# Changed order of preference in the crossing and in attention, and conditioning strips summed through DRAM, in a two-layer hybrid backbone step

## Chip, cores and metric

One core of one Trainium2 chip runs the whole program. The metric is device time in microseconds, from launch to end on that core; a value for a kernel is the median of its runs.

## The reference, cut to what matters

A step of a diffusion backbone over 256 context tokens and 1024 latent tokens of width 1024, two layers: gated linear attention in both directions (GLA), then softmax attention with eight query heads and two key heads. Both layers are modulated by a conditioning vector (`c` for the latent tokens, `c_ctx` for the context):

```python
for l in range(DEPTH):
    mod_p = (jax.nn.silu(c_ctx) @ w_ada[l] + b_ada[l])[None, None, :]
    mod_s = (jax.nn.silu(c) @ w_ada[l] + b_ada[l])[:, None, :]
    sh_p, sc_p, gt_p = split_mod(mod_p)
    sh_s, sc_s, gt_s = split_mod(mod_s)
    hp = rms_norm(xp, norm_g[l]) * (1.0 + sc_p) + sh_p
    hs = rms_norm(xs, norm_g[l]) * (1.0 + sc_s) + sh_s
    ...                      # l = 0: gla_mixer; l = 1: softmax attention, latent keys + cached keys
    xp = xp + gt_p * out_p
    xs = xs + gt_s * out_s
```

So each layer needs 3 x 1024 conditioning values for two vectors: shift, scale and gate.

## The kernel before

All large products are made in three passes of half-precision matmuls (high x high, high x low, low x high; `mm3`, L155), over tiles of 128 tokens. The stages, by the time in the profile:

- **Front** (0 to about 50 us): `x` and 8 MB of `w_ada` come in, the first layer's shift and scale are made (`cond_vectors`, `mod_rows`, `affine(0)`), the first tokens normalised, transposed and modulated into `hT_hi` and `hT_lo`.
- **GLA** (to about 582 us): `gla` runs 50 slots, five rounds (`h` 0 to 4) of ten token tiles. A slot makes a head's decay, states and local products for one tile, the projections ahead (`value_gate`, `qk_piece`), finishes the head before (`combine`, `gated`), and calls `filler(slot)`, which hangs on the rest: the stages of later weights, the conditioning blocks, from slot 30 the output weights, and from slot 42 the first four output tiles. Start and final states and, before, the gate strips share the one tile `s0`.
- **Crossing** (to about 723 us, `gla_out`): output projection and `residual` of the other tiles, the second layer's modulation (`mod_tile`, with rows `gb` from DRAM), keys and values (`key_tile`), first query tiles (`query`, `query_rest`). Each projected tile first needs its row prepared: `out_prep` scales it, splits it and transposes it by DMA into `hT_hi` and `hT_lo`.
- **Attention** (to about 1171 us): ten steps (`n`), each four heads of 256 tokens; the scores of a head come in two halves (`scores` j = 0, 1) over PSUM tile `S`; ScalarE's exponential `p` (L1189), high and low parts `phl`, a DMA transpose into `PT`, and two heads later `values`. Query tiles, their finishing, key tiles and gates lie between.
- **Output** (to the end): `att_out`, the second output projection and its residuals.

**The conditioning blocks.** The 16 blocks of 256 columns that the front leaves over (the first layer's gate, all of the second layer) are loaded at odd slots; the slot after, `gemv` makes eight products in four 32-row strips of the PE array, so the result `m` (128 x 256) holds four partial sums, two rows of each strip being used. The slot after that, `mod_sum` adds the strips on PE against the 0/1 matrix `sel` (L335 for shift and scale, L345 for gates), and VectorE adds the bias (L337, L346); gates go to DRAM (`gt_d`, L347). `affine(1)` at slot 34 scales the second layer's shift and scale, and `affine_rows` transposes them (L372) and stores them (`gb_d`). They are read at slot 40, as rows broadcast to all partitions.

**What sets the order.** The program is written by one thread; a planner then orders each engine's instructions with a timeline of its own. Each instruction has a place in the order of writing, and of the instructions that are ready in that timeline the one with the lowest place goes first. `with k.later("name")` adds `LATER["name"]` to the places of what is written in it: a positive number puts it behind, a negative one ahead. `tc.issue_after(x)` puts instructions behind `x` on its engine. The order planned is fixed in the program; the engines run it in that order and wait where something is late.

Of the kernel before, what the change touches and what calls it, by code (L numbers as in the profile page):

```python
# [12 lines left out]
ALU = mybir.AluOpType  # L13
# [34 lines left out]
    "local": 5,  # L48
    "loc": -30,
    "kt": 30,  # L50
    "A": 10,
    "intra": -5,
    "ks": -85,
# [4 lines left out]
    "gated": 60,  # L58
    "decay": -25,
    "outer": 5,  # L60
    "oa": 220,
    "Uc": -5,
    "pieces8": 10,
# [9 lines left out]
class K:  # L73
# [57 lines left out]
    def mulcol(self, a, b, pool, tag, const=None):  # L131
        o = self.t(pool, [P, 1], F32, tag)
# [53 lines left out]
    def fill_out(self, w, st):  # L186
# [13 lines left out]
        so = self.t(self.small, [P, 2], F32, "wso")  # L200
# [69 lines left out]
    def cond_vectors(self, rows, brow):  # L270
        nc, cp = self.nc, self.const
        ps = self.bank("z")
        nc.tensor.transpose(ps[:, 0:32], rows, self.ident[0:32, 0:32])
        nc.tensor.transpose(ps[:, 32:80], brow, self.ident[0:48, 0:48])
        cT = self.t(cp, [P, 80], F32, "cT")
        nc.vector.tensor_copy(cT, ps[:, 0:80])
        self.gT = cT[:, 16:32]
        self.bT = cT[:, 32:80]
        c = self.t(cp, [P, 16], F32, "silu_c")
# [5 lines left out]
        self.modT = [self.t(cp, [P, 16, 2], F32, f"modT{l}") for l in range(2)]  # L285

    def mod_rows(self, rows):
# [12 lines left out]
        for b in range(4):  # L302
            nc.tensor.transpose(ps[:, b * P : b * P + P], m[:, b * P : b * P + P], self.ident)
        nc.vector.tensor_tensor(
            self.modT[0].rearrange("p (j b) i -> p j b i", j=4),
            ps.rearrange("p (b j r) -> p j b r", b=4, j=4)[:, :, :, 0:2],
            self.bT[:, 0:16].rearrange("p (j b) -> p j b", j=4).unsqueeze(3).to_broadcast([P, 4, 4, 2]), ALU.add,
# [19 lines left out]


    def mod_sum(self, l, b, m):
        nc = self.nc  # L330
        ps = self.bank("mm")
        if b < 8:
            for j in range(2):
                o = 2 * j
                nc.tensor.matmul(ps[:, o : o + 2], m[:, j * P : j * P + P], self.sel[:, 0:2], start=True, stop=True)  # L335
            f = 2 * b
            nc.vector.tensor_tensor(  # L337
                self.modT[l][:, f : f + 2, :], ps[:, 0:4].rearrange("p (f i) -> p f i", i=2),
                self.bT[:, 24 * l + f : 24 * l + f + 2].unsqueeze(2).to_broadcast([P, 2, 2]), ALU.add,
            )  # L340
        else:
            a = 256 * (b - 8)
            r = self.t(self.ew, [P, DV], F32, "s0", bufs=1)[0:2, :]
            nc.sync.dma_start(r, self.I["b_ada"][l : l + 1, 2 * D + a : 2 * D + a + 256].to_broadcast([2, 256]))
            nc.tensor.matmul(ps[0:2, 0:256], self.sel[:, 0:2], m, start=True, stop=True)  # L345
            nc.vector.tensor_tensor(r, ps[0:2, 0:256], r, ALU.add)  # L346
            nc.sync.dma_start(self.gt_d[l, :, a : a + 256], r)  # L347


    def affine(self, l):  # L350
        nc, sp = self.nc, self.const
        mod = self.modT[l]
        gb = self.t(sp, [P, 2, 2, KT], F32, f"gb{l}")
        g, sh = (gb[:, j].rearrange("p i k -> p k i") for j in range(2))
        gT = self.gT[:, 8 * l : 8 * l + 8].unsqueeze(2).to_broadcast([P, KT, 2])
        nc.vector.scalar_tensor_tensor(g, mod[:, 8:16, :], 1.0, gT, ALU.add, ALU.mult)
        m = self.t(self.small, [P, 2], F32, "wmx")
        for j, t in enumerate((mod[:, 0:8, :], g)):
            nc.vector.tensor_reduce(m[:, j : j + 1], t, AX.XY, ALU.max, apply_absolute_value=True)
        mx = self.t(self.small, [P, 1], F32, "af_m", bufs=1)  # L360
        nc.vector.scalar_tensor_tensor(mx, m[:, 1:2], 32.0, m[:, 0:1], ALU.mult, ALU.add)
        s, inv = self.pow2(mx)
        nc.vector.tensor_scalar(sh, mod[:, 0:8, :], s, None, ALU.mult)
        nc.vector.tensor_scalar(g, g, s, None, ALU.mult)
        c = self.t(sp, [P, 1], F32, f"invh{l}")
        nc.vector.tensor_copy(c, inv)
        return gb, g, sh, c


    def affine_rows(self, gb):  # L370
        ps = self.bank("mm")[0:32, 0:P]
        self.nc.tensor.transpose(ps, gb.rearrange("p s i k -> p (s i k)"), self.ident)  # L372
        r = self.t(self.ew, [P, 256], F32, "mod", bufs=1)[0:32, 0:P]
        self.nc.vector.tensor_copy(r, ps)
        self.nc.sync.dma_start(self.gb_d.rearrange("s i (k p) -> (s i k) p", p=P), r)
# [30 lines left out]
    def normalise(self, xs, junk):  # L406
        nc = self.nc
        n = len(xs)
        ssq = self.t(self.sm, [P, n], F32, f"nt_s{n}")
# [79 lines left out]
    def rank_scales(self):  # L489
        nc, inv = self.nc, self.inv_rank  # L490
        inv_r = self.mulcol(self.inv_h, inv[:, 0:1], self.small, "inv_r")
# [3 lines left out]
        one = self.t(self.small, [P, 2], F32, "one")  # L495
# [4 lines left out]
        row = self.mulcol(one[:, 0:1], self.sr, self.small, "one_r")  # L500
        ones = self.r[96:98, :]
        nc.vector.tensor_scalar(ones, ones, row[96:98, :], None, ALU.mult)
        t = self.mulcol(inv_r, one[:, 1:2], self.small, "inv_z")
# [74 lines left out]
    def value_gate(self, h, i, w):  # L578
# [8 lines left out]
        if h > 0:  # L587
            x = self.t(self.ew, [P, DV], F32, "gx")
# [335 lines left out]
    def gla_out(self, wo, early, n0):  # L924
# [3 lines left out]
        self.inv_h = self.mod1[3]  # L928
# [14 lines left out]
        for n in range(n0, NT):  # L943
            i = order[n]
            if n == NT - 1:
                self.query_rest()
                with self.tc.issue_after(self.pe):
                    self.query()
                self.key_tile(order[n - 2], wkv)
                self.query_rest()  # L950
# [14 lines left out]
            self.mod_tile(i, x, (t[:, 0], t[:, 1]), self.last)  # L965
            for j in {3: (0,), 4: (1, 2), 5: (3,), 6: (4,), 7: (5,), 8: (6,)}.get(n, ()):
                self.key_tile(order[j], wkv)
            if n == 8:
                with self.tc.issue_after(self.pe):
                    self.query()  # L970
            if n == n0:
# [9 lines left out]
                with self.tc.issue_after(last):  # L981
                    self.att_setup(*ckv)
                    self.key_setup(*ckv, inv)
# [298 lines left out]
    def attention(self, wo, wk):  # L1282
# [7 lines left out]
        for n, (p, c) in enumerate(self.steps):  # L1290
# [8 lines left out]
            for e in range(4):  # L1299
                h = 4 * p + e  # L1300
                if later:
                    self.nc.sync.dma_start(*later.pop(0))
                PT = self.t(self.sp, [P, 20, 256], F16, "PT", bufs=3)
                self.scores(h, c, 0, q[(p, c, 0)], PT)
                if e % 2 == 0:
                    self.query()
                    self.rest()
                    self.scores(h, c, 1, q[(p, c, 1)], PT)
                else:
                    self.query_rest()  # L1310
                if len(pend) == 2:
                    self.values(*pend[0], g.pop(pend.pop(0)[0]))
                else:
                    self.key_tile(len(pend), wkv)
                if e % 2 == 1:
                    self.scores(h, c, 1, q[(p, c, 1)], PT)
                pend.append((h, c, PT))
                if e % 2 == 1:
                    g.update({i: self.gateT(i, c, *wg[p]) for i in (h - 1, h)})
                    self.rest()  # L1320
# [9 lines left out]
        self.out_tile(OUT[0], 0, self.t(self.sp, [P, TS + PAST], F32, "p")[:, 0:D], wo)  # L1330
        for t in pend:
            self.values(*t, g.pop(t[0]))
# [50 lines left out]
def emit(ctx, tc, I, O, dbg=None, stop=None):  # L1383
# [15 lines left out]
    k.gt_d = k.t(k.dram, [2, 2, D], F32, "gt_d")  # L1399
    k.gb_d = k.t(k.dram, [2, 2, D], F32, "gb_d")  # L1400
# [6 lines left out]
    k.sel = k.t(k.const, [P, 2], F32, "sel")  # L1407
# [5 lines left out]
    with ExitStack() as c:  # L1413
# [5 lines left out]
        k.p2_bank = "z"  # L1419
        banks = ("z", "cs", "A", "kt", "U", "o")  # L1420
        k.gla_init()
        with ExitStack() as c1:
# [3 lines left out]
            rows = k.t(k.p1, [32, P], F32, "rows")  # L1426
            brow = k.t(k.p1, [48, P], F32, "brow")
# [3 lines left out]
            small(rows[16:32, :], I["norm_g"].rearrange("l (k p) -> (l k) p", p=P))  # L1431
            small(brow, I["b_ada"].rearrange("l (k p) -> (l k) p", p=P))
            small(k.sel, I["k_sel"])
# [19 lines left out]
            k.cond_vectors(rows, brow)  # L1453
# [20 lines left out]
            _, k.gs, k.sh, k.inv_h = k.affine(0)  # L1474
# [16 lines left out]
            k.rank_sum(*k.rank(1))  # L1491
        k.tl = k.pool("tl", ctx=c)
# [10 lines left out]
        wo, part, prep, held, xs = [], [], [], [], []  # L1503
# [124 lines left out]
def _constants():  # L1628
# [5 lines left out]
    sel = np.zeros((P, 2), f32)  # L1634
    for j in range(4):
        for i in range(2):
            sel[32 * j + i, i] = 1
# [10 lines left out]
    for p in (pos // 64, pos % 64):  # L1648
# [8 lines left out]
        "k_ident": np.eye(P, dtype=f32), "k_sum3": sum3, "k_sel": sel, "k_cum": np.ascontiguousarray(cum),  # L1657
# [41 lines left out]
```

## Time and profile before

| | us |
|---|---|
| runs of the kernel | 1290.27, 1292.72, 1293.17 (median 1292.72) |
| profiled execution, its own time | 1293.64 |
| its span from first to last instruction | 1291.9 |
| TensorE (PE) busy | 1209.2 |
| VectorE (DVE) busy | 920.0 |
| ScalarE (ACT) busy | 706.0 |
| GpSimd (POOL) busy | 353.3 |
| mean granted clock of TensorE | 0.991 |

PEld is the weight load of TensorE, SP the engine whose queue issues most DMAs. A row of a timeline has start, duration, engine, line, operation, tiles (out<-in) and shape, and in brackets the idle time of the engine just before and what ended it. A row of the waits has who waited for whom, the total, how often and the longest. A row of the busy time by stretch has the stretch, its length, each engine's busy time with the count of instructions, the clock granted to TensorE (1.00 is full), the mean busy share of the 16 DMA engines, and GB/s.

### The profile page before, as it was taken

What the parts mean: (1) busy time and instruction counts of PE and PEld (TensorE: products, weight loads), DVE (VectorE), ACT (ScalarE), POOL (GpSimd) and SP (SyncE); (2) the same over time, 40 slices, a digit from 0 to 9 for tenths busy, and PEclk for the clock granted to TensorE, in tenths of its full rate; (3) what the DMA queues carried; (4) which work ended last, traced back from release to release, by engine and by line L of the source; (5) the groups of instructions that cost most, each with busy time, mean ns of one, the idle gap of its engine ahead of it and who ended that gap; (6) DMA issues with size and microseconds to landing.
All of it is one profiled execution on the core that took longest, in us unless ns stands there. A gap on an engine that the chain in (4) does not pass through costs nothing. (4 is left out here: it accounts for less than half of the span.)

```text
span 1291.9 us, 22221 instructions
## 1 busy us (share of the span) xinstructions
PE 1209.2 (94%) x7936; PEld 778.7 (60%) x7936; DVE 920.0 (71%) x2120; ACT 706.0 (55%) x1706; POOL 353.3 (27%) x594
## 2 busy tenths in 40 slices
PE   3899999999999989897999889999999999989998
PEld 1367666655555546664776557676666767656444
DVE  4676678877778789767676667677767677785552
ACT  2684466756656656642334376666767686673110
POOL 1132113223321243410223334342243345312000
PEclk9999999999999999998999999999999999999999
DMA  9711566455555543459965696667957657879432
GB/s 358 259 34 34 164 199 202 149 166 159 160 158 177 172 127 107 147 138 329 210 143 156 176 200 121 136 135 131 198 116 164 136 106 145 185 138 228 139 143 82
DMA packets 357454, 207.51 MB, mean 161 GB/s; under 512 B 251054, under 2 KB 341438, under 8 KB 354912
## 3 DMA queue, kind: packets, MB, share of 16 engines
q1 hardware_dynamic: 349824, 188.02, 57.1%
q0 software_dynamic: 4080, 12.73, 3.0%
q10 hardware_dynamic: 3440, 5.35, 1.1%
q8 instruction: 62, 1.02, 0.3%
q14 instruction: 48, 0.39, 0.1%
HBM read 107.45 MB, written 37.26 MB: 112 GB/s over the span
## 5 line engine op out<-in xcount | busy, mean ns | idle before, releaser
L155 PEld LDWEIGHTS <-hT_hi 128*128 128x128 f16 x1920 | 188.8, 99 | 124.2 <-issue 12.4
L155 PE MATMUL mm<-whi,hT_hi 128*128 128x512 f16 (+1 forms) x576 | 201.1, 349 | 2.9 <-ACT gx L589 1.8
L155 PE MATMUL mm<-whi,hT_lo 128*128 128x512 f16 (+1 forms) x576 | 200.8, 349 | 0.2 <-DMA hT_lo<-hl 0.2
L155 PE MATMUL mm<-wlo,hT_hi 128*128 128x512 f16 (+1 forms) x560 | 195.0, 348 | 0.0
L1214 DVE SCALAR_TENSOR_TENSOR phl<-p,srec,phl 128x1280 f16<-128x1280 f32 (+1 forms) x80 | 107.6, 1347 | 72.4 <-POOL phl L1211 37.9
L155 PEld LDWEIGHTS <-whi 128*128 128x128 f16 x1232 | 120.1, 98 | 60.8 <-issue 2.4
L155 PE MATMUL mm<-hT_hi,whi 128*128 128x256 f16 (+1 forms) x480 | 141.0, 294 | 0.7 <-DVE s L346 0.7
L155 PE MATMUL mm<-hT_hi,wlo 128*128 128x256 f16 (+1 forms) x480 | 141.0, 294 | 0.0
L155 PE MATMUL mm<-hT_lo,whi 128*128 128x256 f16 (+1 forms) x480 | 141.0, 294 | 0.0
L155 PEld LDWEIGHTS <-hT_lo 128*128 128x128 f16 x960 | 94.5, 98 | 70.0 <-DMA hT_lo<-k 5.4
L1181 PE MATMUL S<-kT,wst 128*128 128x512 f16 (+1 forms) x624 | 122.9, 340 | 12.7 <-ACT p L1189 12.2
L155 PE MATMUL mm<-PT,vh 128*128 128x256 f16 x672 | 112.2, 273 | 9.8 <-DMA PT<-phl 8.0
L1211 POOL TENSOR_SCALAR phl<-p,srec 128x1280 f16<-128x1280 f32 (+1 forms) x40 | 57.2, 1430 | 192.1 <-DVE srec L1205 83.1
L1184 DVE TENSOR_REDUCE smx<-S 128x1 f32<-128x1280 f32 (+1 forms) x80 | 101.5, 1269 | 9.2 <-PE S L1181 9.0
L1189 ACT ACTIVATE p<-S,snb,sexp 128x1280 f32<-128x1280 f32 (+1 forms) x80 | 99.4, 1242 | 5.3 <-DVE phl L1214 1.8
L1181 PEld LDWEIGHTS <-wst 128*128 128x128 f16 x624 | 61.1, 98 | 65.7 <-issue 14.5
L155 PE MATMUL mm<-PT,vl 128*128 128x256 f16 x336 | 91.6, 273 | 0.0
L155 PEld LDWEIGHTS <-wlo 128*128 128x128 f16 x616 | 60.3, 98 | 31.5 <-DVE wlo L1352 1.8
L155 PEld LDWEIGHTS <-vh 128*128 128x128 f16 x672 | 65.1, 98 | 20.7 <-issue 9.4
L1019 POOL TENSOR_TENSOR rope<-hx,ropet 128x64 f32<-128x64 f32 x160 | 63.1, 424 | 32.2 <-ACT hx L1145 16.7
L178 DVE TENSOR_REDUCE wmx<-wst 128x1 f32<-128x512 f32 x104 | 65.0, 676 | 5.9 <-DMA wst<-in_att_w_in 2.5
L1186 ACT ACTIVATE snb<-smx,nsexp 128x1 f32<-128x1 f32 x80 | 23.3, 291 | 75.3 <-DVE smx L1184 73.4
(370 smaller groups left out, 2694.5 us busy)
## 6 DMA issues: line engine op xcount, KB each, us to landing
wada<-in_w_ada SPq DMA_DIRECT2D x16, 1024.0 KB, 5.2
wst<-in_gla_w_in SPq DMA_DIRECT2D x12, 1024.0 KB, 5.0
wst<-in_att_w_in SPq DMA_DIRECT2D x10, 1024.0 KB, 5.5
og_d<-gx SPq DMA_DIRECT2D x40, 128.0 KB, 2.7
og_d<-og POOLq DMA_DIRECT2D x40, 128.0 KB, 3.0
wst<-og_d SPq DMA_DIRECT2D x5, 1024.0 KB
xr<-x_d SPq DMA_DIRECT2D x9, 512.0 KB, 6.4
out<-xr ACTq DMA_DIRECT2D x17, 256.0 KB, 3.0
```

The source lines that it names most:

```text
L155: self.pe = self.nc.tensor.matmul(out, a, b, start=k == 0 and j == 0, stop=k == n - 1 and j == 2).ins
L178: nc.vector.tensor_reduce(mx[:, j : j + 1], st[:, 2 * j : 2 * j + 2, :], AX.XY, ALU.max, apply_absolute_value=True)
L1019: nc.gpsimd.tensor_tensor(tv[:, h, :, w, :], xv[:, h, :, 1 - w, :], sn[:, :, w, :], ALU.mult)
L1181: nc.tensor.matmul(S[:, a : a + n], x, y, start=m == 0, stop=m == 2)
L1184: last = nc.vector.tensor_reduce(mx, S, AX.X, ALU.max).ins
L1186: nc.scalar.activation(nb, mx, AF.Copy, scale=self.nsexp)
L1189: nc.scalar.activation(p, S, AF.Exp, scale=self.sexp, bias=nb, accum_out=den)
L1211: nc.gpsimd.tensor_scalar(hi, p, r, 2.0 ** 14, ALU.mult, ALU.mult)
L1214: nc.vector.scalar_tensor_tensor(lo, p, r2, hi, ALU.mult, ALU.subtract)
```

## The change

Five things.

1. `LATER` has new numbers for most names of the GLA stage and new names for the crossing (`x.`), for attention (`a0.` the first two heads, `a9.` the last step, `a.` the rest) and its end (`z.`); the calls in `gla_out` and `attention` stand in `with self.later(...)`, otherwise as they were.
2. `mod_sum` on PE, `sel` and `affine_rows` are gone. `gemv` stores its strips to a DRAM tensor `md_d`; `mod_load` reads them back regrouped (slot 9 for the first layer's gate, slot 34 for the whole second layer), in pieces of eight floats, and the job of the slot after sums the four strips on VectorE, adds the bias, and stores gate and modulation rows.
3. `cond_vectors` transposes one tile of 40 rows instead of two of 32 and 48: the second layer's vectors no longer pass there.
4. The tile `gx` of `value_gate` has three buffers instead of two. Some small tiles get fewer.
5. In the front, the small products of `pow2` go to PSUM bank `o` instead of `z`.

```diff
 LATER = {
-    "local": 5, "loc": -30, "kt": 30, "A": 10, "intra": -5, "ks": -85,
-    "combine": -15, "cs": -10, "vg": -10, "u": 100, "gated": 60, "decay": -25,
-    "outer": 5, "oa": 220, "Uc": -5, "pieces8": 10,
+    "local": 10, "loc": -25, "kt": 30, "A": -15, "intra": -5, "ks": -100,
+    "combine": -15, "cs": -10, "vg": -10, "u": 100, "gated": 50, "decay": -25,
+    "outer": 15, "oa": 100, "Uc": -100, "pieces8": 30,
+    "gate": -5, "jobs": -10, "filler": -25, "o": 60,
+    "x.q": -100, "x.qr": 100, "x.prep": 150, "x.key": 115, "x.key8": 60,
+    "x.mod": -15, "x.res": -225,
+    "a0.s0": 65, "a0.s1": 400, "a0.key": -100, "a0.qr": -30,
+    "a.s0": -25, "a.s1": 30, "a.q": -210, "a.qr": 150, "a.val": 20,
+    "a9.s1": -160, "a9.q": -105, "a9.qr": 30, "a9.rest": 15, "a9.gate": 30, "z.val": 30,
 }
 def gemv(self, l, b, to):
...
     nc.scalar.copy(m, ps[:, 0:256])
-    return l, b, m
+    nc.sync.dma_start(self.md_d[l, :, 256 * b : 256 * b + 256], m)
+
+def mod_load(self, l, s, n):
+    t = self.t(self.ew, [P, 256], F32, "mod", bufs=1)
+    md = t[:, 0 : 64 * n].rearrange("p (s j i k) -> p s j i k", s=n, j=4, i=2)
+    bias = t[:, 192 : 192 + 8 * n].rearrange("p (s k) -> p s k", s=n)
+    src = self.md_d[l].rearrange("(j r) (s p k) -> s r p j k", r=32, s=3, k=KT)
+    load = self.nc.sync.dma_start
+    for m in range(n):
+        for i in range(2):
+            load(md[:, m, :, i], src[s + m, i])
+    load(bias, self.I["b_ada"][l].rearrange("(s p k) -> p s k", s=3, k=KT)[:, s : s + n])
+    if n == 3:
+        load(t[:, 216:224], self.I["norm_g"][l].rearrange("(p k) -> p k", k=KT))
+    return l, md, bias, t[:, 216:224]
-def mod_sum(self, l, b, m):
...
-            nc.tensor.matmul(ps[:, o : o + 2], m[:, j * P : j * P + P], self.sel[:, 0:2], start=True, stop=True)
...
-        nc.tensor.matmul(ps[0:2, 0:256], self.sel[:, 0:2], m, start=True, stop=True)
-        nc.vector.tensor_tensor(r, ps[0:2, 0:256], r, ALU.add)
-        nc.sync.dma_start(self.gt_d[l, :, a : a + 256], r)
+def mod_sum(self, md, bias, tag):
+    n = md.shape[1]
+    m = self.t(self.const, [P, n, 2, KT], F32, tag)
+    for a in range(n):
+        nc.vector.tensor_reduce(m[:, a], md[:, a].rearrange("p j i k -> p i k j"), AX.X, ALU.add)
+    nc.vector.tensor_tensor(m, m, bias.unsqueeze(2).to_broadcast([P, n, 2, KT]), ALU.add)
+    return m
+
+def gate_store(self, l, m):
+    self.nc.sync.dma_start(self.gt_d[l].rearrange("i (p k) -> p i k", k=KT), m)
+
+def mod_rows_out(self, l, md, bias, gn):
+    m = self.mod_sum(md, bias, "mod1")
+    self.gate_store(l, m[:, 2])
...      # scale and shift fitted to a power of two as in affine
+    for j in range(2):
+        self.nc.sync.dma_start(self.gb_d[j].rearrange("i (p k) -> p i k", k=KT), gb[:, j])
...
 def value_gate(self, h, i, w):
-        x = self.t(self.ew, [P, DV], F32, "gx")
+        x = self.t(self.ew, [P, DV], F32, "gx", bufs=3)
...
 def gla_out(self, wo, early, n0):
-            last = self.residual(i, lambda k: (hT[:, k, :], lT[:, k, :]), wo, inv, x)
+            with self.later("x.res"):
+                last = self.residual(i, lambda k: (hT[:, k, :], lT[:, k, :]), wo, inv, x)
...
-                    prep[order[n + 2]] = self.out_prep(*rows.pop(n + 2))
+                    with self.later("x.prep"):
+                        prep[order[n + 2]] = self.out_prep(*rows.pop(n + 2))
...
 def attention(self, wo, wk):
+                at = ("a0." if n == 0 and e < 2 else "a9." if n == 9 else "a.")
...
-                    self.query()
+                    with self.later(at + "q"):
+                        self.query()
...
 def filler(slot):
-            if part:
-                k.mod_sum(*part.pop())
+            if slot in (9, 34):
+                gm.append(k.mod_load(*((0, 2, 1) if slot == 9 else (1, 0, 3))))
+            if slot in (10, 35):
+                k.jobs.append(((k.gate_rows if slot == 10 else k.mod_rows_out), *gm.pop()))
             if slot % 2 == 0:
                 if held:
-                    part.append(k.gemv(*held.pop()))
+                    k.gemv(*held.pop())
...
-            if slot == 34:
-                k.jobs.append((lambda: setattr(k, "mod1", k.affine(1)),))
-            if slot == 35:
-                k.jobs.append((k.affine_rows, k.mod1[0]))
```

More of the change, by code (lines that the diff above doesn't have):

```diff
@@ L57 @@
     "u": 100,
-    "gated": 60,
+    "gated": 50,
     "decay": -25,
[L60 to L63, printed above, removed]
+    "outer": 15,
+    "Uc": -100,
+    "a9.qr": 30,
+    "a.s1": 30,
+    "gate": -5,
+    "a0.key": -100,
+    "x.qr": 100,
+    "z.val": 30,
+    "o": 60,
+    "x.q": -100,
+    "a0.qr": -30,
+    "x.prep": 150,
+    "x.key": 115,
+    "a9.rest": 15,
+    "oa": 100,
+    "jobs": -10,
+    "a.q": -210,
+    "x.mod": -15,
+    "x.res": -225,
+    "a.val": 20,
+    "a9.gate": 30,
+    "a9.q": -105,
+    "a.s0": -25,
+    "a.qr": 150,
+    "a9.s1": -160,
+    "a0.s1": 400,
+    "pieces8": 30,
+    "filler": -25,
+    "x.key8": 60,
+    "a0.s0": 65,
 }
@@ L366, in affine @@
         nc.vector.tensor_copy(c, inv)
[L367 to L375, printed above, removed]
+        return g, sh, c
     def rows_load(self, i):
@@ L964, in gla_out @@
                 self.rows_load(0)
-            self.mod_tile(i, x, (t[:, 0], t[:, 1]), self.last)
+            with self.later("x.mod"):
+                self.mod_tile(i, x, (t[:, 0], t[:, 1]), self.last)
             for j in {3: (0,), 4: (1, 2), 5: (3,), 6: (4,), 7: (5,), 8: (6,)}.get(n, ()):
-                self.key_tile(order[j], wkv)
+                with self.later("x.key"):
+                    self.key_tile(order[j], wkv)
             if n == 8:
                 with self.tc.issue_after(self.pe):
-                    self.query()
+                    with self.later("x.q"):
+                        self.query()
             if n == n0:
@@ L1329, in attention @@
         wo[:] = [(hi, lo, 512) for hi, lo, _ in wo]
-        self.out_tile(OUT[0], 0, self.t(self.sp, [P, TS + PAST], F32, "p")[:, 0:D], wo)
+        with self.later("z.out"):
+            self.out_tile(OUT[0], 0, self.t(self.sp, [P, TS + PAST], F32, "p")[:, 0:D], wo)
         for t in pend:
-            self.values(*t, g.pop(t[0]))
+            with self.later("z.val"):
+                self.values(*t, g.pop(t[0]))
     def out2_load(self, c):
@@ L1656, in _constants @@
     return {
[L1657 removed]
+        "k_ident": np.eye(P, dtype=f32), "k_sum3": sum3, "k_cum": np.ascontiguousarray(cum),
         "k_mask": np.ascontiguousarray(mask), "k_rope": np.ascontiguousarray(rope),
```

164 lines of the change are left out of this document (85 added, 79 removed).

## The prediction, made before the changed kernel was run

> **What bounds the kernel now.** I read the page first, then busy time by stage, the list of what TensorE (PE) waited for, and the timeline where a wait or a removed instruction lies.
>
> ```profile
> span 1291.9 us, 22221 instructions
> PE 1209.2 (94%) x7936; PEld 778.7 (60%) x7936; DVE 920.0 (71%) x2120; ACT 706.0 (55%) x1706; POOL 353.3 (27%) x594
> ```
>
> The span is 1291.9 us; the profiled execution took 1293.64, the median of the three is 1292.72. I work from 1293.64 and take off the 0.9 at the end. PE is busy for 94%, so 82.7 us of idle PE is all that a better order can win, unless PE is given less to do. The busy time of each engine by stage:
>
> ```profile
> core 0: us, PE busy (x) PEld busy (x) DVE busy (x) ACT busy (x) POOL busy (x), PEclk, DMA share, GB/s
> 0.00:50.00 50.00, 23.36 (x114) 9.99 (x115) 28.96 (x79) 18.83 (x32) 5.45 (x12) 0.97 1.00 366
> 50.00:450.00 400.00, 395.74 (x2482) 238.57 (x2480) 302.59 (x803) 243.28 (x601) 102.71 (x187) 1.00 0.48 147
> 450.00:582.00 132.00, 120.68 (x757) 80.80 (x750) 104.48 (x285) 77.48 (x202) 46.69 (x77) 0.97 0.45 129
> 582.00:723.00 141.00, 131.68 (x964) 94.93 (x963) 101.63 (x230) 47.51 (x118) 38.86 (x74) 0.98 0.80 203
> 723.00:766.00 43.00, 34.49 (x236) 22.99 (x234) 27.33 (x48) 22.70 (x55) 11.18 (x18) 0.98 0.96 207
> 766.00:1125.00 359.00, 351.74 (x2518) 245.79 (x2517) 260.46 (x531) 251.46 (x629) 133.00 (x208) 1.00 0.70 143
> 1125.00:1171.00 46.00, 37.72 (x292) 28.15 (x290) 38.53 (x58) 29.15 (x52) 8.02 (x8) 1.00 0.77 170
> ```
>
> From 50 to 450 (linear attention) PE is busy 395.7 of 400: there an instruction taken from PE is time taken from the kernel. The first 50 us are DMA's (share 1.00). The rest of the idle time is 11 us at the end of the linear attention, 9 in the crossing (582 to 723), 8.5 at the start of attention, 7 in its middle and 8 in its last step. Some of those that PE waited for, over the whole span (total, times, longest):
>
> ```profile
> PE mm L155 <- DMA PT<-phl: 8.0, 6, 1.9
> ...
> PE y L155 <- DMA hT_lo<-k: 4.9, 1, 4.9
> PE kv L113 <- DVE amx L1076: 4.1, 1, 4.1
> ...
> PE mm L155 <- ACT gx L589: 1.8, 4, 0.6
> ...
> PE mm L155 <- DVE s L346: 1.1, 2, 0.7
> ```
>
> **Strips over DRAM: what PE no longer does.** `mod_sum` added up the four 32-row strips of each conditioning block on PE against the 0/1 matrix `sel`; now the strips go to DRAM, come back regrouped, and DVE adds them. Eight blocks took the column form (four short passes each), eight the row form (two passes); one transpose in `affine_rows` goes too. PE is pipelined, so I price them from start to next start:
>
> ```profile
> 201.91 0.50 PE L335 MATMUL mm<-sel,mod 128*128 128x2 f32 x4
> 202.28 0.68 PE L676 MATMUL U<-v,ks 128*128 128x256 f32 x2
> ...
> 119.16 0.59 PE L345 MATMUL mm<-mod,sel 128*2 128x256 f32 x2
> 119.69 0.23 PE L629 MATMUL cs<-cum,ghi 128*128 128x130 f16 x1
> ...
> 498.24 0.42 PE L372 MATMUL mm<-ident,gb 128*32 128x128 f32 x1
> 498.45 0.63 PE L155 MATMUL mm<-whi,hT_hi 128*128 128x512 f16 x1
> ```
>
> 8 x 0.37 + 8 x 0.53 + 0.21 = 7.4 us of PE time. It lies where PE is full, so it counts whole: -7.4. With `mod_sum` goes PE's wait for its DVE addition (`DVE s L346`, 1.1 us above): -1.1. The row form also sat in tile `s0`, of which there is one, which the scan's start states use too:
>
> ```profile
> 444.98 0.25 SPq L347 DMA_DIRECT2D gt_d<-s  x1
> ...
> 449.66 0.34 SPq L711 DMA_DIRECT2D out<-s  x1
> 451.38 4.08 SPq L698 DMA_DIRECT2D s<-in_state_gla  x2
> ```
>
> ```profile
> PE A L722 <- POOL Sa L699: 1.4, 1, 1.4
> ...
> PE o L736 <- POOL Sc L699: 0.9, 1, 0.9
> ```
>
> At 445 the gate strip leaves `s0`, then a final state, then two start states come in, and PE waits 0.9 and 1.4 us for them. Between nothing and 2.3 us can come back; the final state and the two loads still share the one tile, so I take the low third, -0.7. Strips together: -9.2.
>
> **What the strips add.** DVE gets four small reductions and two additions for sixteen additions: no more than it had, off the path. SP's queue loses 17 transfers (8 bias loads, 8 gate stores, one `gb_d` store) and gains 31: 16 strip stores of 128 KB, 11 loads, 4 small stores. The loads come in pieces of eight floats, 32 bytes: eight strip loads of 512 pieces, with bias, norm and the four stores about 5760 small pieces, and 2048 for the strip stores.
>
> ```profile
> q1 hardware_dynamic: 349824, 188.02, 57.1%
> ...
> og_d<-gx SPq DMA_DIRECT2D x40, 128.0 KB, 2.7
> ```
>
> 57.1% of 16 engines' span over 349,824 packets is 34 ns a packet, so 7800 of them take about 16 us of all engines; from 50 to 450 their share is 0.48, so there is room. A read-back waits on SP for the landing of the last store (2.7 us, from the 128 KB row). Behind it in SP's queue stand `og_d` stores, weight stages and start states. The results are needed only at slots 40 and later, from rows made at slots 11 and 36, so I put the DMA side at nothing; if its cover is gone it costs up to those 16 us, which is a rival below. `mod` is a single tile that the read-back shares with the next block's copy: once, at slot 10, a PSUM bank may be held for a slot, 0 to 2 us; I take 0, since the next block's products are due no earlier than slot 40.
>
> **Third buffer for the gate tile.** `gx` in `value_gate` gets three buffers instead of two. PE's 1.8 us on `ACT gx` comes from a buffer whose store had not landed:
>
> ```profile
>   DMA og_d<-gx: 3.2, 3
> ```
>
> That is what ScalarE waited for ahead of L589 from 505 to 550. The buffer can bring 1.8; but next late there is the state recurrence over POOL and DVE, which PE waits for in the same stretch:
>
> ```profile
> PE o L736 <- POOL Sc L701: 1.6, 1, 1.6
> ```
>
> I take half, -1.0. The smaller changes (`p2_bank` "o" in the front, one conditioning load fewer) lie in the DMA-bound first 50 us: 0, at most -1.
>
> **Crossing: residuals ahead (-225), key tiles (+115) and row preparation (+150) behind.** The offsets change only which of several ready instructions the planner takes. The first wait, 4.9 us for `hT_lo`, has nothing else on PE to put there (the key weights are only just being loaded), and DMA is past full around it:
>
> ```profile
> 585.00:594.00 9.00, 4.09 (x13) 1.47 (x12) 5.19 (x16) 1.07 (x2) 0.54 (x1) 0.81 1.21 301
> 601.00:611.00 10.00, 5.87 (x41) 4.48 (x39) 9.60 (x19) 2.47 (x5) 1.14 (x2) 0.83 1.06 382
> ```
>
> The second, for `amx`, has a key tile behind it and then the next `hT_lo`:
>
> ```profile
> 606.04 0.23 PE L113 MATMUL kv<-ident,amx 128*128 128x128 bf16 x1 [4.13 <-DVE amx L1076]
> ...
> 614.14 0.39 PE L155 MATMUL y<-whi,hT_lo 128*128 128x512 f16 x1 [0.29 <-DMA hT_lo<-oghl]
> ```
>
> Without the `amx` wait PE would reach 614 four microseconds early and wait for the transpose instead. So I take 0 for the crossing, between -9.0 (both waits go) and the price of the slower rival below.
>
> **Start of attention (723 to 766).** `a0.s1` +400 holds the second half of the scores of the first two heads back and `a0.key` -100 brings key tiles forward: work put exactly where PE waits for ScalarE's exponentials to free `S`.
>
> ```profile
> PE S L1181 <- ACT p L1189: 7.0, 2, 3.5
> ```
>
> Busy time, granted clock (third from the end) and DMA share around the two:
>
> ```profile
> 734.00:742.00 8.00, 4.33 (x32) 2.83 (x30) 4.92 (x7) 4.88 (x12) 2.68 (x4) 1.00 1.00 252
> 759.00:767.00 8.00, 4.12 (x18) 1.90 (x17) 5.30 (x9) 6.64 (x18) 3.03 (x5) 0.82 0.89 123
> 767.00:771.00 4.00, 4.00 (x19) 1.82 (x18) 4.00 (x6) 2.97 (x7) 1.51 (x3) 0.94 1.00 199
> ```
>
> Two waits of 3.5 us. After the second the granted clock is 0.82 over 8 us and 0.94 over 4: 0.18 x 8 + 0.06 x 4 = 1.7 us of clock lost; after the first none. I take one wait and the lost clock, 3.5 + 1.7 = -5.2, within 0 and -8.7: key tiles pulled into the first gap are missing at the second. [...]
>
> **Middle and last step.** From 766 to 1125 the idle 7.3 us is scattered; `a.q` -210 brings query tiles forward, `a.qr` +150 puts their finishing back. I see no direction: 0, within 5 either way. In the last step the query tiles are used up:
>
> ```profile
> PE S L1181 <- ACT p L1189: 4.9, 4, 1.7
> PE mm L155 <- DMA PT<-phl: 3.4, 2, 1.7
> ```
>
> `a9.s1` -160 starts second halves of scores sooner and `z.val` +30 leaves the last values behind the output tile as cover: of these 8.3 us I take -3.0, within -8.3 and +4.
>
> **Sum.** -9.2 - 1.0 + 0 - 5.2 + 0 - 3.0 = -18.4; 1293.64 - 18.4 = 1275.2, on the median's scale 1274.3. Forecast 1275.
>
> **Rivals.** (1) The strips bring their 9.2 and the new order gives as much as it takes: 1283.5, with 1279 to 1290 around it. For it: waits on DMA and on ScalarE stay whatever the order. (2) The small pieces hold SP's queue: their 16 us stand in front of start states and stores that PE waits for, 18.4 - 16 leaves 1290 to 1293, no change. Against it: slack from slot 11 to 40 and a DMA share of 0.48. [...] No run shown here has 32-byte pieces in number. (3) Slower: the crossing starves. Row preparation set behind makes `hT_lo` late for each of the six tiles prepared there (ten less the four early ones), as it was once, 4.9 us. 6 x 4.9 = 29 us more, less 18.4: 1304. It decides from four late tiles on (4 x 4.9 = 19.6). For it: key tiles, the only other work there, are put behind the residuals, so none is held for a late transpose at a fixed place. Against it: the stage's idle time, 141.0 - 131.7 = 9.3 us, is those first two waits and 0.3, so later preparation had time in hand. (4) Slower: query tiles drawn ahead leave the values uncovered, so that they wait for `PT`: 8.0 / 6 = 1.3 us each; half of the 40 value groups are 27 us, 1302. Against it: one such wait a step at most so far. That the change does nothing is excluded by PE's 7.4 us.
>
> **How the numbers follow.** Forecast 0.50 (1262 to 1284 for itself: with gate buffer and attention at their good ends 9.2 + 1.8 + 8.7 + 5.0 + 8.3 = 33 us, about 1261; with the strips alone 1284), rival 1 0.22, rival 2 0.05, rival 3 0.14, rival 4 0.09. What can be told from no change here is about 0.2%, 2.6 us: faster means under 1290.1. Faster 0.72, same 0.05, slower 0.23. The range: 1260 leaves out under 0.05 below, 1302 about half of rivals 3 and 4 above, 0.12.
>
> **What would show it.** Right: no `sel` matmuls, PE busy time about 7 us lower, 50 to 450 shortened by that; one wait on `ACT p` of 3.5 at the start of attention gone and its slow clock with it; `hT_lo` wait at the crossing's begin still there. Wrong: linear attention no shorter, or with new waits on start states or `gx`; new PE waits on `hT_lo<-oghl` in the crossing; waits on `PT<-phl` above 8 us in all.

## The result and the profile after

The changed kernel takes 1274.75 us (median of four runs, 1273.22 to 1276.68), the kernel before 1292.95 beside it: a ratio of 0.9858 with a 95% interval of 0.9838 to 0.9878, or 18.2 us less. The profiled execution took 1276.0 us, its span is 1274.2. The forecast was 1275 and the sum 18.4. The total is right; the terms of which it was made are largely not, and the rest of this document is about that.

The head of the page of the kernel after:

```profile
span 1274.2 us, 22158 instructions
PE 1194.7 (94%) x7886; PEld 776.6 (61%) x7886; DVE 926.2 (73%) x2109; ACT 694.4 (54%) x1706; POOL 339.8 (27%) x594
...
DMA packets 365454, 209.72 MB, mean 165 GB/s; under 512 B 257110, under 2 KB 349438, under 8 KB 362912
```

Fifty matmuls are gone (eight blocks of four, eight of two, two transposes), and PE is busy 14.5 us less, twice what was expected. Next, busy time by stage, cut in both kernels at the same landmarks instead of at fixed times: the first time tile `U` is written (transposes of `x` at the end of the front), the first product of the output projection (`y`), the first and the last score (`S`). The columns are as in the prediction. Before:

```profile
core 0: us, PE busy (x) PEld busy (x) DVE busy (x) ACT busy (x) POOL busy (x), PEclk, DMA share, GB/s
0.00:61.20 61.20, 33.31 (x159) 14.49 (x160) 35.26 (x95) 28.57 (x47) 7.71 (x15) 0.97 0.90 325
61.20:574.30 513.10, 498.77 (x3139) 310.25 (x3138) 396.20 (x1061) 306.70 (x778) 143.85 (x255) 0.99 0.47 142
574.30:723.30 149.00, 139.68 (x1015) 99.81 (x1013) 106.49 (x243) 51.84 (x126) 42.14 (x80) 0.98 0.80 201
723.30:1163.20 439.90, 417.57 (x2985) 291.25 (x2982) 319.31 (x624) 299.76 (x728) 151.48 (x232) 1.00 0.73 150
1163.20:1291.90 128.70, 119.85 (x647) 62.87 (x646) 62.78 (x103) 19.15 (x27) 8.11 (x12) 0.99 0.48 147
```

After:

```profile
0.00:57.90 57.90, 31.09 (x159) 13.98 (x160) 34.64 (x96) 28.69 (x47) 7.70 (x15) 0.97 0.94 344
57.90:553.30 495.40, 486.36 (x3089) 307.58 (x3088) 393.29 (x1052) 303.36 (x777) 144.48 (x257) 1.00 0.50 153
553.30:727.50 174.20, 150.90 (x1084) 107.20 (x1084) 114.40 (x250) 54.30 (x132) 40.34 (x80) 0.93 0.83 192
727.50:1146.10 418.60, 406.73 (x2914) 285.10 (x2913) 321.22 (x615) 288.48 (x724) 138.09 (x229) 1.00 0.76 147
1146.10:1274.20 128.10, 119.62 (x647) 62.72 (x644) 62.59 (x99) 19.56 (x27) 9.19 (x13) 0.99 0.50 148
```

Front 3.3 us shorter, linear attention (GLA) 17.7 shorter, crossing 25.2 longer, attention 21.3 shorter, output 0.6 shorter. Part of the last two exchanges is work that moved: 69 matmuls more in the crossing, 71 fewer in attention (key and query tiles now run before the first score). Idle PE, the stretch less PE's busy time, tells more: GLA 14.3 to 9.0, crossing 9.3 to 23.3, attention 22.3 to 11.9. So the changed kernel lost 14 us of PE in the crossing. Its 23.3 us are nearly all two rows of what PE waited for: 19.7 for `amx`, once, and 3.5 for a key weight (`PT<-w_kv`, at 717, just ahead of the first score):

```profile
PE kv L139 <- DVE amx L1125: 19.7, 1, 19.7
PE mm L181 <- DMA PT<-phl: 4.9, 4, 2.0
PE S L1230 <- ACT p L1238: 4.5, 6, 2.3
PE mm L181 <- DMA PT<-w_kv: 3.5, 1, 3.5
PE mm L181 <- ACT gx L627: 3.3, 3, 2.2
...
PE mm L181 <- ACT gx L1273: 2.1, 1, 2.1
```

### The profile page after: what moved, and what is told of

The parts are those of the page before. It is cut to its first block, busy times and chain, and to the rows that moved or that the text cites. A ratio compares the mean times of both kernels' runs of the same rounds, so it can differ in the third digit from the quotient of the medians.

```text
span 1274.2 us, 22158 instructions
## 1 busy us (share of the span) xinstructions
PE 1194.7 (94%) x7886; PEld 776.6 (61%) x7886; DVE 926.2 (73%) x2109; ACT 694.4 (54%) x1706; POOL 339.8 (27%) x594
## 5 line engine op out<-in xcount | busy, mean ns | idle before, releaser
L1230 PE MATMUL S<-kT,wst 128*128 128x512 f16 (+1 forms) x624 | 139.5, 338 | 4.5 <-ACT p L1238 4.5
L181 PE MATMUL mm<-PT,vh 128*128 128x256 f16 x672 | 115.0, 275 | 5.6 <-DMA PT<-phl 4.9
L1260 POOL TENSOR_SCALAR phl<-p,srec 128x1280 f16<-128x1280 f32 (+1 forms) x40 | 53.7, 1343 | 105.9 <-DMA PT<-phl 55.9
L1068 POOL TENSOR_TENSOR rope<-hx,ropet 128x64 f32<-128x64 f32 x160 | 53.3, 363 | 76.6 <-ACT hx L1194 65.5
L172 POOL TENSOR_TENSOR hrs<-hrsa,mhalf 128x2 f32<-128x2 f32 x50 | 39.9, 800 | 74.6 <-DVE hrsa L170 74.1
```

Of the source, the lines that this page charges most:

```text
L172: nc.gpsimd.tensor_tensor(r, a, self.mhalf[:, 0:w], ALU.pow)
L181: self.pe = self.nc.tensor.matmul(out, a, b, start=k == 0 and j == 0, stop=k == n - 1 and j == 2).ins
L1068: nc.gpsimd.tensor_tensor(tv[:, h, :, w, :], xv[:, h, :, 1 - w, :], sn[:, :, w, :], ALU.mult)
L1230: nc.tensor.matmul(S[:, a : a + n], x, y, start=m == 0, stop=m == 2)
L1260: nc.gpsimd.tensor_scalar(hi, p, r, 2.0 ** 14, ALU.mult, ALU.mult)
```

## Experiments

**Which half brings it: the strips or the order?** Two kernels, each with one half. `strips_only` is the changed kernel with the numbers of before and none of the new names; `orders_only` is the kernel before with all the new numbers and names.

```diff
 # strips_only, from after (the new names x. a0. a. a9. z. go too)
-    "local": 10, "loc": -25, "A": -15, "ks": -100, "gated": 50, "outer": 15, "oa": 100, "Uc": -100, "pieces8": 30, ...
+    "local": 5, "loc": -30, "A": 10, "ks": -85, "gated": 60, "outer": 5, "oa": 220, "Uc": -5, "pieces8": 10,
 # orders_only, from before: the same lines the other way, with the calls in `with self.later(...)`
```

> The changed kernel with the 16 old numbers of LATER back and none of the new names: strips through DRAM, third gate buffer, bank o in the front, and the old order. If the strips are worth what PE no longer does (7.4 us of matmuls, 1.1 of waits on the addition, 0.7 of start states, 1.0 for the gate buffer), 1283, with 0 to 450 shorter by 8 to 9 us and the waits on ACT p at the start of attention as before. If the gain of the change is the order alone, 1291 to 1293.

> The kernel before with the new numbers and names of LATER in all three stages, but with mod_sum on PE, two gate buffers, and bank z. If strips and order add up, 1274.75 + 9.2 = 1284. If the new order in the linear attention is what shortened it, and PE's 7 us were room that it had anyway, 1276 to 1278.

`strips_only` measured 1284.9 us, 0.9931 (0.9907 to 0.9956); `orders_only` 1288.57, 0.9947 (0.9929 to 0.9965). Each half brings about half: 0.69% and 0.53%, together 1.22 of the 1.42%, which the intervals allow to be plainly additive. Both came out slower than expected for halves that add up, by 1.9 us (1283) and by 4.6 (1284). And the first half is three edits at once, taken apart further on. The new numbers of the GLA stage bring nothing there: cut as above, GLA takes 514.2 us in `orders_only` against 513.1:

```profile
61.70:575.90 514.20, 496.89 (x3138) 311.25 (x3137) 397.49 (x1067) 305.75 (x780) 140.83 (x255) 0.99 0.47 142
```

**The new names of the crossing, and those of attention.** From the changed kernel, either group left out.

```diff
 # no_cross
-    "x.q": -100, "x.qr": 100, "x.prep": 150, "x.key": 115, "x.key8": 60, "x.mod": -15, "x.res": -225,
 # no_att
-    "a0.s0": 65, "a0.s1": 400, "a0.key": -100, "a0.qr": -30, "a.s0": -25, "a.s1": 30, "a.q": -210, "a.qr": 150, "a.val": 20,
-    "a9.s1": -160, "a9.q": -105, "a9.qr": 30, "a9.rest": 15, "a9.gate": 30, "z.val": 30,
```

> The changed kernel without the seven x. names, so the crossing in the order of before. If the 19.7 us wait on DVE amx comes of residuals ahead and preparation behind, it is back at about 4 and the time is 1264 to 1268. If the wait comes of the end of the linear attention having become shorter, while the loads into the crossing take as long as ever, it stays above 12 and the time is 1273 to 1280, the gain of the other x. names gone.

> The changed kernel without the a0., a., a9. and z. names: attention in its order of before. If the order in attention is worth the difference that the traces show from the first score to the last output, less the key and query tiles that moved ahead of the first score, 1282 to 1288, with two waits on ACT p of some 3.5 us back. If those tiles moved by the x. names alone, and attention gains only by their absence, 1275 to 1278.

`no_cross` measured 1275.09 us, 0.9846 (0.9822 to 0.987): the names of the crossing are worth nothing that shows. `no_att` measured 1285.48, 0.9933 (0.9901 to 0.9964): those of attention are worth about 10 us (its profiled execution was the longest of its runs, 1291.18, so its rows serve for kinds of waits only).

**Why PE stands for 19.7 us.** PE finishes with the first output tile and has only a key tile's finishing left, whose maximum `amx` is late. From the timeline of the kernel after, by engine (PE, DVE, SP's queue, ACT):

```profile
574.03 0.27 PE L181 MATMUL y<-wada,hT_lo 128*128 128x256 f16 x1
593.97 0.29 PE L139 MATMUL kv<-ident,amx 128*128 128x128 bf16 x1 [19.66 <-DVE amx L1125]
...
591.38 0.29 DVE L1124 TENSOR_REDUCE amx<-qn 128x1 f32<-128x128 f32 x1 [9.03 <-DMA hT_lo<-split]
...
578.79 3.47 SPq L441 DMA_TRANSPOSE hT_lo<-split  x1
...
591.46 1.06 ACT L427 ACTIVATE hl<-xr 128x1024 f16<-128x1024 f32 x1 [13.54 <-DMA hT_lo<-split]
```

The reduction that makes `amx` does not read `split` or `hT_lo`, yet it ends its wait together with that transpose: the two are tied by a place in memory. The pools of the crossing are opened on SBUF that GLA has just left, and `amx` in pool `sm3` lies (at byte 193,088 of each partition) inside GLA's last `split` tile (190,528 to 194,624). Two DMA transposes read that tile, and the later one, issued at 578.8, lands only at about 591. ACT's row `hl` (13.5 us) ends its wait with the same transpose. VectorE runs nothing between 582.4 and 591.4, so all that it has behind the reduction stands for the 9.0 us too; PE runs nothing between 574.3 and 594.0, and in its order nothing else comes before the product that wants `amx`. `sm_first` opens `sm3` before two others, so that its small tiles land elsewhere, off `split`; `before_sm_first` does it to the kernel before; `amx_own` moves that one tile alone to another pool.

```diff
 # sm_first (before_sm_first: the same three lines in the kernel before)
+            k.sm = k.pool("sm3", bufs=4, ctx=c)
             k.xp = k.pool("x3", ctx=c)
             k.hw = k.pool("hw3", bufs=2, ctx=c)
-            k.sm = k.pool("sm3", bufs=4, ctx=c)
 # amx_own, from after
-        m = self.t(self.sm, [P, 4], F32, "amx", bufs=1)
+        m = self.t(ap, [P, 4], F32, "amx", bufs=1)
```

> The changed kernel with the crossing's pool of small tiles opened ahead of its two other pools, so that amx and the row sums lie where a tile lay that was done long before, and no longer on the last split tile of the linear attention. If the 19.7 us wait is a wait for that place (the transposes of split land at about 591), the wait on amx falls to 8 to 10 us, VectorE being free at 582, some of it comes back as a wait on hT_lo, and the time is 1266 to 1271. If amx waits for its own loads (query and key norm, caches), the wait stays at 17 to 20 and the time at 1275.

> The changed kernel with amx alone in the attention's own pool; the row sums of the crossing stay on the split tile. If the place of amx is all that PE waits for, as sm_first: amx wait 8 to 10 us, 1266 to 1271. If the row sums, which stand on the same engines and wait for the same place, hold VectorE or the key tiles, 1271 to 1275.

> The kernel before with the same swap of pools. There the wait on amx was 4.1 us and the next hT_lo came at 614 whatever PE did: if the crossing is bound by its loads, the time falls by 0 to 3 us (1290 to 1293), a wait on hT_lo taking the place of the one on amx. If the place of the small tiles held the whole crossing back, it falls by 5 or more.

`sm_first` measured 1270.75 us (1268.55 to 1272.56), 0.9811 (0.9789 to 0.9832): faster than both kernels, 4.0 us below the changed one by the medians. What PE waited for in the crossing of `sm_first`, its reduction, and busy time in the crossing and in attention:

```profile
PE kv L139 <- DVE amx L1125: 8.7, 1, 8.7
```

```profile
L1124 DVE TENSOR_REDUCE amx<-qn x1: 279/279/279, 582.7 to 582.7; 128x1 f32<-128x128 f32 x1
```

```profile
553.70:709.50 155.80, 146.37 (x1060) 104.58 (x1060) 109.76 (x241) 53.93 (x131) 39.55 (x77) 0.97 0.86 206
709.50:1139.10 429.60, 412.29 (x2938) 288.74 (x2937) 326.34 (x624) 288.82 (x726) 138.61 (x233) 0.99 0.74 146
```

The reduction itself now runs at 582.7 instead of 591.4, neither it nor ScalarE's `hl` ends a wait with that transpose any more, and the idle time of the crossing falls from 23.3 to 9.4 us. So the place was worth 11.0 of the 19.7 us. Of the other 8.7 the profile of `sm_first` shows this: from 566 VectorE works nearly without a break on output tiles that stand before the reduction in its order; just before, it stood 5.7 us for ScalarE's pass into the next `split`, and ScalarE 5.5 us for the transposes that read the `split` before it (there is one buffer). A second buffer was not tried. Of the 14 us less in the crossing 4.0 reach the end: 24 of the moved matmuls are back in attention, and its idle time is 17.3 us where the changed kernel has 11.9. `amx_own` shortens the wait too, but not the time:

```profile
PE kv L139 <- DVE amx L1125: 12.7, 1, 12.7
```

1275.44 us, 0.9859 (0.9826 to 0.9891). So the one tile is not all, and two rows of `amx_own` show what else is tied:

```profile
DVE sv_i L1153 <- DMA hT_lo<-split: 3.5, 1, 3.5
```

```profile
ACT hl L427 <- DMA hT_lo<-split: 7.7, 1, 7.7
```

`sv_i`, and the row sums that ACT's pass over `hl` leaves for the next output tiles, are in `sm3` too and still lie on `split`; in `sm_first`, where all of `sm3` is moved, both rows are gone. `before_sm_first` measured 1295.22, 1.0011 (0.9991 to 1.0032): in the kernel before the same swap brings nothing. The tie stood there as well, in the rows of VectorE and ScalarE of the profile before:

```profile
DVE amx L1078 <- DMA hT_lo<-split: 6.6, 1, 6.6
```

```profile
ACT hl L389 <- DMA hT_lo<-split: 10.8, 1, 10.8
```

But little hung on it. With the swap VectorE stands 5.3 us for the next `og` row instead, the reduction of `qn` runs at 602.7 instead of 605.3, and PE's waits on `hT_lo` and `amx` are still 4.2 and 3.5 us (4.9 and 4.1 before). That the tie costs more in the changed kernel because its crossing starts 21 us sooner fits this, but was not tested by itself.

**What the names of the crossing are worth once that wait is short.** `sm_first` without the seven `x.` names.

> The swap of pools and no x. names. If the x. names are worth nothing either way, as no_cross says, 1270 to 1272 like sm_first. If residuals ahead and preparation behind only pay once the wait on amx is short, it is slower: 1273 to 1277.

1274.26 us, 0.9853 (0.9825 to 0.9881), against 1270.75 and 0.9811 (0.9789 to 0.9832) with them. The two intervals overlap a little; 3.5 us for the names is likely, not shown.

**Strips, gate buffer and bank taken apart.** `strips_pure` is `strips_only` with two `gx` buffers and bank `z`: of the change only the strips over DRAM. `gx2` and `bank_z` are the changed kernel with one of those edits undone.

```diff
 # gx2 (strips_pure too)
-        x = self.t(self.ew, [P, DV], F32, "gx", bufs=3)
+        x = self.t(self.ew, [P, DV], F32, "gx")
 # bank_z (strips_pure too)
-        k.p2_bank = "o"
+        k.p2_bank = "z"
```

> The changed kernel with the old LATER, two gate buffers and bank z: of the change only the strips and the smaller small tiles. If the strips alone make the gain of strips_only (8.9 us), 1284 to 1286. If the third gate buffer is worth the 1.0 us that was put down for it and bank o the 3 us by which the front ended sooner, 1288.

> The changed kernel with two gate buffers again. If the third buffer is worth the 1.0 us put down for it, 1275 to 1277, and PE waits on ACT gx in the linear attention 1 to 3 us longer. If it makes the 4.7 us by which the linear attention of strips_only is shorter than that of strips_pure, 1279 to 1281.

> The changed kernel with the small products of pow2 in bank z again in the front. If the front gains from bank o and what follows keeps it, the first state product on PE comes 3 to 4 us later (61 to 62 instead of 57.9) and the time is 1277 to 1279. If the crossing's loads take the gain back, the front is later and the time stays 1274 to 1276.

`strips_pure` measured 1295.97 us, 1.0013 (0.9991 to 1.0036): no change, though the matmuls are gone, and slower than either expectation. Its GLA, crossing and attention:

```profile
62.90:562.70 499.80, 483.43 (x3066) 306.06 (x3065) 394.98 (x1053) 304.39 (x779) 142.12 (x255) 1.00 0.50 151
562.70:717.50 154.80, 138.31 (x1015) 99.30 (x1013) 104.38 (x235) 51.15 (x126) 44.23 (x80) 0.94 0.79 192
717.50:1162.30 444.80, 422.59 (x2985) 294.06 (x2982) 319.18 (x621) 299.63 (x728) 148.05 (x232) 0.98 0.74 148
```

(The front of `strips_pure` holds 23 matmuls more by this cut, so its GLA holds fewer than the fifty account for.) The crossing starts at 562.7 instead of 574.3 and ends at 717.5 instead of 723.3. Half of the gain is lost there, and one PE wait of `strips_pure` says at what:

```profile
PE y L155 <- DMA hT_hi<-oghl: 14.1, 1, 14.1
```

The row of the next output tile is not there yet. The rest goes in attention, 4.9 us longer, where the same 2985 matmuls are busy 422.59 us instead of 417.57, at a mean granted clock of 0.98 instead of 1.00, and in the output, 1.4 us longer. The lower clock is not an accident of the profiled execution: over the whole span it is 0.976 to 0.985 in the ten runs of `strips_pure`, and 0.983 to 0.992 in the 19 of the kernel before beside them.

`gx2` measured 1284.29, 0.9936 (0.991 to 0.9961): the third buffer is worth 9.5 us in the changed kernel, more than either expectation. Its GLA, 503.2 us against 495.4, with 15.8 us of idle PE against 9.0:

```profile
58.10:561.30 503.20, 487.36 (x3090) 307.24 (x3089) 396.48 (x1055) 303.20 (x777) 141.41 (x254) 0.99 0.50 150
```

What ScalarE waited for to write `gx`, from 300 to 575 us, first in the kernel before, then after, in `gx2` and in `strips_pure`:

```profile
ACT gx L589 <- DMA og_d<-gx: 4.2, 6, 1.8
```

```profile
ACT gx L627 <- DMA og_d<-gx: 3.9, 4, 1.8
```

```profile
ACT gx L627 <- DMA og_d<-gx: 10.0, 9, 2.7
```

```profile
ACT gx L601 <- DMA og_d<-gx: 18.4, 9, 6.1
```

With two buffers ScalarE's wait goes from 4.2 us to 10.0 and 18.4 in the two kernels that give PE less to do. PE itself waits little for `gx` in `gx2` (0.3 us from 450 on); its largest wait in GLA is elsewhere, on GpSimd's state recurrence:

```profile
PE z L774 <- POOL Sc L739: 4.6, 1, 4.6
```

Ahead of that step GpSimd scales four weight pieces (`wst`, 3.6 us), which had waited 0.6 us for ScalarE. How ScalarE's wait on the buffer comes to cost PE time is not shown step by step. Nor is the buffer parted from the order: with another number of buffers the planner writes out another one.

`bank_z` measured 1278.52, 0.9877 (0.9841 to 0.9913); the interval overlaps that of the changed kernel. The front shows it: the first product of `U` comes at 62.9 us, as in `strips_pure`, and at 57.9 with bank `o`. That is 5.0 us of the stage; by the medians 3.8 reach the end, which the intervals do not show. In the front the transposes of `x` go through bank `z` too, and wait there until VectorE has copied the one before to `xT`. The wait in the kernel before, of which the changed kernel has 0.4 us left and `bank_z` 4.6:

```profile
PE z L420 <- DVE xT L1458: 3.9, 3, 2.3
```

**The start of attention.** The four `a0.` names alone left out.

```diff
 # no_a0
-    "a0.s0": 65, "a0.s1": 400, "a0.key": -100, "a0.qr": -30,
```

> The changed kernel without the four a0. names: the first two heads of attention in the old place. If they remove one wait of 3.5 us and a slow clock, as put down (5.2), 1279 to 1281. If the gain of attention's order is spread over its steps, 1275 to 1277.

1275.09 us, 0.9854 (0.9827 to 0.9881): these names are worth nothing that shows, and without them no wait of 3.5 us on `ACT p` comes back (five in all of attention, 4.0 us, the longest 2.2). The 10 us of the attention names are thus in `a.`, `a9.` and `z.`, as long as those stand.

## Why the prediction came out, step by step

**Strips, -9.2: the saving is there, its price was not.** PE's products are gone as counted (fifty matmuls, priced at 7.4 us), and GLA, with the gate buffer and the new order as well, is even 17.7 us shorter. Of that, 12.4 is busy time: the 7.4, about 1.2 of slow clock (an estimate from busy time and granted clock: 0.79 over 464 to 472 and 496 to 504 before, 0.79 over 510 to 518 after), 1.4 less over the same 256 products of `gemv` (the rows below, before and after), and some 2.4 that I can't place; 5.3 is idle time.

```profile
L320 PE MATMUL mm<-wada,cst 128*32 128x256 f32 x256 | 22.2, 386 | 0.0
```

```profile
L344 PE MATMUL mm<-wada,cst 128*32 128x256 f32 x256 | 20.8, 386 | 0.0
```

The step failed in "it counts whole": less work for a full PE in one stage made the next stage start sooner; by how much that one ended sooner was set by its own waits (11.6 us sooner at its start, 5.8 at its end, in `strips_pure`). By themselves the strips brought 0 (`strips_pure`), because the crossing then waits for its rows (14.1 us) and attention runs at a lower clock (0.98 against 1.00). The prediction's first rival put the strips alone at 1283.5; with the gate buffer and the bank they reach 1284.9, without them 1296.

**Third gate buffer, -1.0: measured -9.5.** The size was read from PE's wait, 1.8 us, and bounded by it. That was the wrong engine's row. It is ScalarE that fills the buffer, whose wait on it was 4.2 us before and rises to 10.0 and 18.4 when PE no longer holds ScalarE back. In the changed kernel PE's own wait on `ACT gx` is even longer (3.3 us) and the kernel still gains. That the buffer would bring little without the strips is likely from these rows, but was not run.

**Front, 0: about -4.** "DMA-bound" was taken from a share of 1.00. But the bank that the transposes share with the small products counted too: with another bank the stage was 3.3 us shorter, at a DMA share of 0.94 (0.90 before, by the same cut).

**Crossing, 0: right in sum, wrong in every part.** The `hT_lo` wait was to stay; it went. The `amx` wait was to be exchanged for another; it became 19.7 us, 11.0 of them through a tie in memory. The prediction went by PE's rows alone; the tie was in the profile before, in the 6.6 and 10.8 us that VectorE and ScalarE stood for `hT_lo<-split`. Without the names of the crossing it is still 15.7 us (`no_cross`), and the names measure 0. Rival 3, a crossing starved of transposed rows, did happen in kind in `strips_pure` (one row late by 14.1 us) and not six times.

**Start of attention, -5.2: wrong cause.** Both 3.5 us waits on `ACT p` went instead of one, but a wait on the key weights took 3.5 (`PT<-w_kv` in the rows above) and one on a gate 2.1; and the names to which the gain was put are worth nothing. The case against it, that key tiles pulled forward move the gap, is what happened. The stretch of slow clock at the start is gone (1.00 from 727.5 to 780), but one as long stands in the last step of the changed kernel:

```profile
1123.50:1131.50 8.00, 6.01 (x41) 4.66 (x41) 7.41 (x10) 4.41 (x6) 1.35 (x2) 0.79 0.63 125
```

So the 1.7 us of clock were not won, only moved (0.21 x 8 = 1.7). In `strips_pure`, with the old order and waits of 3.6 and 2.4 us on `ACT p` at the start, the clock is 0.58 over 729.5 to 737.5 and 0.79 over 755.5 to 763.5; in the kernel before it was 1.00 at the first of the two waits (734 to 742) and 0.82 at the second (759 to 767). So in these rows a wait of about 3.5 us goes with a slow clock at one place and with a full one at another; what decides between them was not shown. Why the ten runs of `strips_pure` have the lower clock nearly throughout is open.

**Middle 0, last step -3.0: the gain was here.** Over all of attention, two of PE's waits, before and then after:

```profile
PE S L1181 <- ACT p L1189: 12.2, 7, 3.5
...
PE mm L155 <- DMA PT<-phl: 6.3, 5, 1.9
```

```profile
PE S L1230 <- ACT p L1238: 4.5, 6, 2.3
...
PE mm L181 <- DMA PT<-phl: 4.1, 3, 2.0
```

These two sum up to some 10 us less, but about half of that is the start, where other waits took their place. With all waits that PE's rows list, the start goes from 8.4 us (723 to 766) to 7.2 (700 to 770, the 3.5 on the key weights included), the middle from 7.4 (to 1125) to 4.8 (to 1100), the last step from 8.3 (to 1171) to 3.3 (to 1156). So it was 1.2 where 3.5 of waits had been put down, 2.6 where 0, and 5.0 where 3.0; `no_att` says that about 10 us is what the names are worth in all. Query tiles drawn ahead did not uncover the values (rival 4: waits on `PT` fell).

**Small pieces (rival 2): no.** The read-backs of 16 KB land in 4.2 us against 5.2 for the 128 KB stores:

```profile
md_d<-mod SPq DMA_DIRECT2D x16, 128.0 KB, 5.2
mod<-md_d SPq DMA_DIRECT2D x8, 16.0 KB, 4.2
```

Per byte that is over six times slower (how much of either time is fixed was not measured), and PE has no wait on it. There are 8000 packets more, as counted, and GLA's DMA share goes from 0.47 to 0.50.

**Sum.** -18.4 against -18.2 is luck of terms. Against the measured parts the prediction had 9 too much for the strips, and too little for the gate buffer (8.5), the front (4) and attention (2.5). These parts were measured against different kernels (0 for the strips alone, -9.5, -3.8 and -10.7 for the others taken out of the changed kernel) and come to -24, not -18: what a part is worth depends on which others are there. How they share the gain further is open; the buffer without the strips, and the strips with buffer and old bank, were not run.

## What to carry to other kernels

When an edit takes work from the bound engine, look at once at what the next stage loads and transposes: unless that comes sooner as well, the saving can turn into a wait there, as it did in `strips_pure` (14.1 us). Price a buffer by the waits of the engine that fills it, and think of them as they will be when its neighbour is faster. And where an engine's wait ends with a DMA on a tile that its instruction does not use, look at where its own tiles lie, on the engines off the critical path as well: opening a pool earlier, so that its tiles lay elsewhere, brought 4 us in the changed kernel and nothing in the kernel before.

## What the runs showed that was not expected

A pool of small tiles, `amx` of 16 bytes a partition among them, held up TensorE for 11.0 of 19.7 us, because it lay on a tile that a DMA transpose was still reading. And the gap cost little clock. Busy time and granted clock around it, in the kernel after:

```profile
570.00:578.00 8.00, 4.30 (x40) 3.61 (x37) 7.27 (x24) 2.31 (x3) 0.54 (x1) 1.00 1.18 304
578.00:586.00 8.00, 0.00 (x0) 0.00 (x0) 4.32 (x5) 0.00 (x0) 0.54 (x1) 0.60 1.17 209
586.00:594.00 8.00, 0.03 (x1) 0.04 (x1) 2.07 (x9) 2.19 (x4) 0.65 (x2) 0.50 1.06 321
594.00:602.00 8.00, 8.00 (x53) 5.66 (x54) 7.24 (x24) 3.46 (x6) 0.47 (x1) 0.83 0.76 184
```

The clock is at half for most of the gap, where no product runs (0.50 from 580 to 594), and only the first part of the 8 us after it is slow (0.50 from 594 to 596, 1.00 from 598): 0.17 x 8 = 1.4 us lost to a wait of 19.7, no more than the 1.7 that the prediction worked out for a wait of 3.5 in the kernel before.
